# A fused retention, sparse-attention and SwiGLU layer: two low halves of token sums by VectorE instead of by transfer, one gate product on another engine, and denser side work

## The chip, the cores and the metric

The kernel runs on one core of a Trainium2 chip. The metric is the device time of one execution in microseconds (us). The engines are TensorE (PE in the profile; PEld is its weight load), VectorE (DVE), ScalarE (ACT), GpSimd (POOL), and SyncE (SP), which here only issues transfers. Each runs its own instructions in the order in which they were emitted. Transfers run on 16 DMA engines that all queues share.

## What is computed

One layer over 512 tokens of width 1024. The input is projected to the parts of a retention group (rq, rk, rv, rg), of an attention group (aq, ak, av), and of an indexer (iq, ik, iw) that picks the 128 keys of each query. The part that matters here:

```python
proj = x @ w_in
rq, rk, rv, rg, aq, ak, av, iq, ik, iw = jnp.split(proj, IN_SPLITS, axis=-1)
...
ret = retention_chunkwise(rq, rk, rv)             # rope on rq, rk before
ret = ((ret - mu) * lax.rsqrt(var + LN_EPS)).reshape(B, S, RET_WIDTH)
ret = (ret * ret_gn_gain.astype(jnp.float32)).astype(x.dtype)
ret = jax.nn.silu(rg) * ret
...
sel = indexer_topk(iq, ik, iw, topk)
att = sparse_attention(aq, ak, av, sel).reshape(B, S, ATT_WIDTH)
mix = jnp.concatenate([ret, att], axis=-1) @ w_out
x = layer_norm(DEEPNORM_ALPHA * x + mix, ln_mix_gain, ln_mix_bias)
gate, up = jnp.split(x @ w_gate_up, 2, axis=-1)
ffn = (jax.nn.silu(gate) * up) @ w_down
return layer_norm(DEEPNORM_ALPHA * x + ffn, ln_ffn_gain, ln_ffn_bias)
```

## The kernel before

**Number format.** Every large product is made of three matmuls in a rounded 32-bit format: each operand is split into a high half (the rounded value) and a low half (the rest), and `mm3` adds high x high, high x low and low x high (lines 94 to 96). `split` makes the halves. The high half is always a copy on ACT (line 86). The low half is made in one of two ways: an engine that is given subtracts (line 91), or, with `None`, ACT writes the negated source (line 88) and POOL issues a transfer that adds the source to it (line 89, an accumulating transfer of 0.5 MB between two places of SBUF for a half-block).

**Stages.** First the indexer's projection, then sixteen feature projections (`proj_feature`, tiles `pf`), then `token_pair`, which makes rv and rg, then `proj_token` (av, tiles `pt`), then the output projection `mix_part` (tiles `mx`) with attention between its matmuls, layer norm, the FFN in two stages, and the last layer norm.

**`token_pair`.** rv and rg are not projected plainly. Tokens and depth are cut in halves, and seven block products stand for eight: p = 0 to 6 use the token blocks 11, 12, the sums s1, s4, s2, s3, and the block 22, with weight blocks that are sums as well. The products are collected in PSUM tiles X (`ptx`), Z (`ptz`) and Y (`pty`); `after(p, t)` copies or adds a finished one out of PSUM. The fourth product (p = 3) is added in PSUM onto the third (both in Y), behind ACT's copy of the third (line 436).

The token sums are made by `x_sums` on POOL (line 390, four subtractions or additions of 128x1024). `x_split` makes the halves of a sum: s1 and s4 during the feature projections, s2 and s3 during the products p = 2 and p = 3. s2 has its own form with the low half on DVE (lines 405, 406); s1, s4 and s3 go through `split(None, ...)`, that is, by transfer.

**Weights.** `stream` lists the weight blocks; each gives two half-blocks, w0, w1, w2 and so on in order of use: w16 and w17 belong to the first block product, w18 and w19 to the second, and so on up to w28 and w29; w30 to w33 are `proj_token`'s. `weight()` prepares them three ahead. Letters say who makes the low half: V is DVE, G is POOL, Q is the transfer. w16, w17: Q, Q. w18 and w19: V, V. w20 to w25: G and V in turn. w26, w27: G, Q. w28, w29: G, V. Three buffers hold raw blocks, so a load waits until an earlier block has been split. The sums of weight blocks are made by accumulating transfers from memory into a raw block (`from_memory`, line 282), which POOL issues after particular half-blocks have been prepared.

**Side work.** `run(main, *sides)` advances side generators each time the main one yields. `pace(it, r)` gives r units of credit at each yield; a step of a side generator costs what it yields. `side` is the chain of the indexer's rope, its logits, the top-k selections (`topk`, lines 511 and 512: one step is a max of eight and a replacement on DVE; the last block's sixteen steps cost 1.6 units each), the token sums and their splits. `rets` is the list of retention steps; `tail` is its rest and then the first attention block's softmax (`att_score(0)`). During `proj_token` `tail` runs at 1.6 and `side` at 0.8; during the first quarter of the output projection `side` runs at 0.6 and is then drained.

**Retention's gate.** For each of four token blocks b, `gated(b)` applies silu on ACT (line 420) and multiplies by the gain on POOL (line 421); `ret_gate(b)` multiplies the normalised retention by it on POOL (line 638, tile `rzz`); `ret_turn(b)` transposes the result on PE (line 645, tile `rz`) and `put_mix` splits it (lines 559, 560).

**Attention's banks.** The scores of one query block are four PSUM tiles `as` (line 669), read by a DVE reduction each (line 671); the tag has four banks, and the transposes `apt` (line 690) take the next ones in turn.

Of the kernel before, what the change touches and what calls it, by code (L numbers as in the profile page):

```python
# [13 lines left out]
ALU = mybir.AluOpType  # L14
# [39 lines left out]
def hybrid_layer_kernel(ctx: ExitStack, tc: tile.TileContext, xT, x, pos, w0, wf, wt, wo,  # L54
                        wgu, wd, gng, lmg, lmb, lfg, lfb, ident_d, cols_d, masks_d, decay_d, out):
    nc = tc.nc
    V, A, G, T = nc.vector, nc.scalar, nc.gpsimd, nc.tensor
# [9 lines left out]
    def psd(name):  # L67
        return psp.tile([P, 512], F32, tag="d", name=name)
# [7 lines left out]
    def unit(tag, name, dt=F32):  # L76
        return big.tile([P, 4, S], dt, tag=tag, name=name)
# [7 lines left out]
    def split(eng_lo, hi, lo, src):  # L85
        A.copy(hi, src)  # L86
        if eng_lo is None:
            A.activation(lo, src, AF.Copy, scale=-1.0)  # L88
            nc.gpsimd.dma_start(lo.bitcast(F32), src, accum_op=ALU.add)  # L89
        else:  # L90
            eng_lo.tensor_tensor(lo, src, hi.bitcast(F32), op=ALU.subtract)  # L91

    def mm3(acc, lh, ll, rh, rl, first, last, **kw):
        T.matmul(acc, lhsT=lh, rhs=rh, start=first, stop=False, **kw)  # L94
        T.matmul(acc, lhsT=lh, rhs=rl, start=False, stop=False, **kw)  # L95
        T.matmul(acc, lhsT=ll, rhs=rh, start=False, stop=last, **kw)  # L96
# [211 lines left out]
    def weight(ahead=3):  # L308
        k = taken[0]
        taken[0] += 1  # L310
        while len(ready) < min(k + 1 + ahead, 2 * limit[0]):
            prepare()
        return ready[k]
# [6 lines left out]
    gnb = const.tile([P, S], F32, name="gnb")  # L320
# [8 lines left out]
    def settle():  # L329
        while pending:  # L330
            pending.pop(0)()
# [24 lines left out]
    def proj_token():  # L356
        accs = [psd(f"pt{b}") for b in range(NB)]

        def evac(b):
            if b == 0:  # L360
                tok[0] = unit("s4", "av")
            A.copy(tok[0][:, b], accs[b])

        for c in range(4):
            h, l = weight()
            for b in range(NB):
                bs = slice(b * P, b * P + P)
                for k in range(2):
                    kt = 2 * c + k
                    ks = slice(k * S, k * S + S)  # L370
                    mm3(accs[b], xh[kt][:, bs], xl[kt][:, bs], h[:, ks], l[:, ks], kt == 0, kt == KT - 1)
                settle()
                if c == 3:
                    pending.append(lambda b=b: evac(b))
                if b != 1:
                    yield

    xq, xs = {}, {}
# [22 lines left out]
    def x_split(q, tag):  # L401
        xs[q] = big.tile([P, 2, 4, T2], F32R, tag=tag, name=f"x{q}")
        hi, lo = xs[q][:, 0], xs[q][:, 1]
        if q == "s2":
            A.activation(hi, xq["n2"], AF.Copy, scale=-1.0)
            V.scalar_tensor_tensor(lo, in0=xq["n2"], scalar=-1.0, in1=hi.bitcast(F32), op0=ALU.mult, op1=ALU.subtract)
        else:
            split(None, hi, lo, xq[q])

    def x_side(q):  # L410
        if q in ("11", "12", "22"):
# [5 lines left out]
    grg = {}  # L417

    def gated(b):
        A.activation(grg[b], grg[b], AF.Silu)  # L420
        G.tensor_tensor(grg[b], grg[b], gnb, op=ALU.mult)

    def token_pair():
        X = [psd(f"ptx{t}") for t in range(2)]
# [25 lines left out]
        for p, (q, first) in enumerate((("11", True), ("12", True), ("s1", True), ("s4", False), ("s2", False), ("s3", False), ("22", False))):  # L450
            if p == 1:
                d4 = big.tile([P, 4, HEADS * P], F32, tag="s7", name="decay")
                rt["decay"] = d4[:, :2]
                dma(rt["decay"], decay_d)
                grg[2], grg[3] = d4[:, 2], d4[:, 3]
            if p == 2:
                Y += [psd(f"pty{t}") for t in range(2)]
            bank = {1: Z, 2: Y, 3: Y}.get(p, X)
            side_of = x_side(q)
            settle()  # L460
            for u in range(2):
                h, l = weight()
                for t in range(2):
                    for k in range(2):
                        hi, lo = side_of(2 * u + k, t)
                        ks = slice(k * S, k * S + S)
                        mm3(bank[t], hi, lo, h[:, ks], l[:, ks], first and u == 0 and k == 0, u == 1 and k == 1,
                            skip_group_check=True)
                    settle()
                    if u == 1:  # L470
                        pending.append(lambda p=p, t=t: after(p, t))
                    if (p, u, t) == (2, 0, 0):
                        x_split("s2", "s10")
                    elif (p, u, t) == (3, 0, 0):
                        x_split("s3", "s4")
                    yield
# [40 lines left out]
    def chain(*its):  # L517
        for it in its:
            yield from it

    def pace(it, r, credit=0.0):
        while True:
            credit += r
            while credit > 0.0:
                c = next(it, 0.0)
                credit -= 1.0 if c is None else c
                if c == 0.0:
                    break
            yield

    def run(main, *sides):
        for _ in main:
            for s in sides:
                next(s, None)

    def drain(it):
        for _ in it:
            pass
# [109 lines left out]
    def retention():  # L648
        steps = (((ret_keys, 0),), ((ret_score, 0),), ((ret_keys, 1),), ((ret_state, 0),), ((ret_score, 1), (ret_decay, 1)), ((ret_out, 0, 0),),
                 ((ret_out, 0, 1),), ((ret_state, 1),), ((ret_keys, 2),), ((ret_score, 2), (ret_decay, 2)), ((ret_out, 1, 0),),  # L650
                 ((ret_out, 1, 1), (ret_scale, 0)), ((ret_state, 2),), ((ret_score, 3), (ret_scale, 1), (gated, 0)), ((ret_out, 2, 0), (ret_gate, 0)),
                 ((ret_out, 2, 1), (gated, 1)), ((ret_out, 3, 0), (gated, 2), (ret_gate, 1)), ((ret_out, 3, 1), (gated, 3)), ((ret_turn, 0), (ret_scale, 2)),
                 ((ret_gate, 2),), ((ret_turn, 1),), ((ret_scale, 3),), ((ret_gate, 3), (ret_turn, 2)), (), (), ((ret_turn, 3),), ())
        for step in steps:
            for f, *a in step:
                f(*a)
            yield
# [4 lines left out]
    def att_score(b):  # L662
        n = (b + 1) * P
        bias = masks[:, 1] if b == 0 else score[:, b, :n]
        mx = sp.tile([P, 4, 4], F32, tag="mx", name="mx")
        st, ex = [], []
        for h in range(HEADS):
            sc = psu(f"as{b}_{h}")
            T.matmul(sc[:, :n], lhsT=aqT[:, h, b * P:n], rhs=akT[:, h, :n], start=True, stop=True)
            st.append(tmp("ast"))  # L670
            V.tensor_tensor_reduce(out=st[h][:, :n], in0=sc[:, :n], in1=bias, scale=1.0, scalar=-3.0e38,
                                   op0=ALU.add, op1=ALU.max, accum_out=mx[:, 0, h:h + 1])
        V.tensor_scalar(mx[:, 1], mx[:, 0], -ATT_SCALE, None, op0=ALU.mult)
        yield
        for h in range(HEADS):
            A.activation(st[h][:, :n], st[h][:, :n], AF.Exp, scale=ATT_SCALE, bias=mx[:, 1, h:h + 1],
                         accum_out=mx[:, 2, h:h + 1])
        yield
        V.reciprocal(mx[:, 3], mx[:, 2])
        for h in range(HEADS):  # L680
            V.tensor_scalar(st[h][:, :n], st[h][:, :n], mx[:, 3, h:h + 1], None, op0=ALU.mult)
            at[b, h] = st[h]
        yield
# [28 lines left out]
    def x_parts():  # L712
        x_load("s8", "11", "22")
        yield 0.01

    def some(it, n):
        for _ in range(n):
            yield next(it)

    def splits(*a):  # L720
        x_split(*a)
        yield 0.5

    def x_sums_in():
        for _ in x_sums():
            pass
        yield 0.01

    def both(main, it, every):
        for n, c in enumerate(main):  # L730
            yield c
            if n % every == every - 1:
                yield next(it)

    lg1, lg23 = logits(1), chain(logits(2), logits(3))
    side = chain(index_rope(), lg1, both(lg23, tk, 2), x_parts(), some(tk, 3), x_sums_in(), some(tk, 3), splits("s1", "s4"), some(tk, 1), splits("s4", "s6"), tk)
# [5 lines left out]
    def later(it, n):  # L742
        for _ in range(n):
            yield
        yield from it
# [1 line left out]
    run(token_pair(), pace(side, 0.8), later(pace(some(rets, 12), 0.65), 10))  # L747
    mixt[0] = unit("s8", "mrh", F32R), unit("s10", "mrl", F32R)
    tail = chain(rets, att_score(0))
    run(proj_token(), later(pace(tail, 1.6), 1), pace(side, 0.8))  # L750
    drain(tail)


# [885 lines left out]
    for i in range(18):  # L1639
        q, j = WORDER[i]  # L1640
# [97 lines left out]
    b = NB - 1  # L1738
# [82 lines left out]
```

## Time and profile before

| what | value |
|---|---|
| time, median of 3 runs | 618.75 us (618.7 to 619.94) |
| the profiled execution: its own time, its span | 618.67 us, 616.9 us |
| PE busy, PEld busy | 601.8 us (98%), 514.4 us (83%) |
| DVE, ACT, POOL busy | 523.5 us (85%), 372.1 us (60%), 199.5 us (32%) |
| software DMA queue (issued by POOL) | 40.05 MB, 37.3% of the 16 engines' span |
| hardware DMA queue (issued by SP) | 84.10 MB, 38.8% |
| `token_pair` on PE | 124.2 to 177.6 us |
| `proj_token` on PE | 177.6 to 210 us |

A busy share is an average over stages with different limits; what a change in one stage is worth is read from the waits in that stage. In the lists of instructions the first number is the start in us, the second the length in us, and a bracket at the end gives the idle time before the instruction and what ended it. A matmul's end is modelled, so neighbouring matmuls overlap in the list. In the list of waits stand the total, the number and the longest. A view of one tile or line gives the shortest, median and longest duration in ns. A row of a transfer gives who issued it, its size, and the us from issue to landing.

### The profile page before, as it was taken

To read this page: it belongs to the slowest core of one execution; us is meant where nothing else is said; L and a number is where in the kernel's file an instruction comes from. 1 tells how busy PE (TensorE), PEld (TensorE's weight loads), DVE (VectorE), ACT (ScalarE), POOL (GpSimd) and SP (SyncE) were. 2 spreads that over 40 slices of the span, in tenths; PEclk is the share of its full clock that TensorE was granted. 3 is DMA by queue.
4 is the path that set the end of the run, shared out by engine and by line. 5 is a ranking of instruction groups with operands and counts; after the bars stand their busy time and mean duration, and the time that the engine had idled before them with its cause. 6 is when DMAs were issued, how large, how long until landed. Compare 5 with 4: busy or idle time off the path is not lost.

```text
span 616.9 us, 9139 instructions
## 1 busy us (share of the span) xinstructions
PE 601.8 (98%) x3204; PEld 514.4 (83%) x3204; DVE 523.5 (85%) x962; ACT 372.1 (60%) x646; POOL 199.5 (32%) x202
## 2 busy tenths in 40 slices
PE   9999999998999999999999999999999999999995
PEld 6988888876788877889998888888888888688884
DVE  5897798998847897889998999999999898887856
ACT  5645554526484765777657767767776695548300
POOL 1188234956678000232123223132221021214011
PEclk9999999998999999999999999999999999999998
DMA  8799898699894673497399988988876559779602
GB/s 306 280 212 263 207 234 223 151 247 275 199 232 119 265 273 135 109 238 152 120 267 204 242 213 211 230 191 236 199 205 177 139 159 229 187 198 302 202 35 102
DMA packets 45790, 125.98 MB, mean 204 GB/s; under 512 B 4736, under 2 KB 12480, under 8 KB 39984
## 3 DMA queue, kind: packets, MB, share of 16 engines
q1 hardware_dynamic: 25312, 84.10, 38.8%
q0 software_dynamic: 19696, 40.05, 37.3%
q10 hardware_dynamic: 736, 1.25, 0.6%
q8 instruction: 25, 0.41, 0.3%
q14 instruction: 21, 0.17, 0.1%
HBM read 91.30 MB, written 2.10 MB: 151 GB/s over the span
## 4 chain that ended last, share of the span: by engine, by line
PE 81%; DMA 7%; DVE 5%; issue 3%; POOL 2%; ACT 1%; POOLq 0%; SPq 0%; DVEq 0%
PE ga L1050 11%; PE ga L1053 6%; PE gc L1050 5%; PE pf L94 5%; PE pf L95 5%; PE pf L96 5%; PE acc L210 4%; PE gb L1050 3%; PE gc L1053 3%; PE ga L1060 3%; DMA raw<-in_wt_dram 2%; PE mx L96 2%; PE mx L94 2%; PE mx L95 2%; DMA xs<-xqs 2%
## 5 line engine op out<-in xcount | busy, mean ns | idle before, releaser
L86 ACT CAST wh<-raw 128x1024 fp32r<-128x1024 f32 x49 | 51.1, 1049 | 42.0 <-DMA raw<-in_wt_dram 11.8
L94 PE MATMUL pf<-xh,wh 128*128 128x512 f32 x128 | 50.0, 391 | 0.0
L95 PE MATMUL pf<-xl,wh 128*128 128x512 f32 x128 | 49.9, 390 | 0.0
L96 PE MATMUL pf<-xh,wl 128*128 128x512 f32 x128 | 49.8, 389 | 0.0
L549 POOL TENSOR_TENSOR rs<-ve,half 128x1 f32<-128x1 f32 (+1 forms) x11 | 11.8, 1068 | 95.5 <-DVE ve L548 95.4
L91 DVE TENSOR_TENSOR wl<-raw,wh 128x1024 fp32r<-128x1024 f32 x24 | 31.7, 1333 | 8.0 <-ACT wh L86 7.9
L89 POOL DMA_DIRECT2D wl<-raw x20 | 19.2, 961 | 40.2 <-ACT wl L88 40.0
L96 PEld LDWEIGHTS pf<-xh,wl 128*128 128x128 f32 x128 | 24.0, 188 | 5.2
L94 PEld LDWEIGHTS pf<-xh,wh 128*128 128x128 f32 x128 | 24.0, 188 | 4.7
L975 POOL DMA_DIRECT2D firsts<-in_wgu_dram x18 | 21.2, 1191 | 20.7 <-DMA firsts<-in_wgu_dram 20.7
L95 PEld LDWEIGHTS pf<-xl,wh 128*128 128x128 f32 x128 | 24.1, 188 | 4.6
L89 POOL DMA_DIRECT2D slot<-hu x9 | 10.9, 1447 | 50.9 <-ACT slot L88 26.8
L511 DVE MAX8 m<-score 128x8 f32<-128x256 f32 (+2 forms) x48 | 26.6, 555 | 0.6
L512 DVE MATCH_REPLACE8 score<-m,score 128x256 f32<-128x256 f32 (+2 forms) x48 | 26.0, 543 | 0.0
L494 ACT ACTIVATE lg<-lg 128x256 f32<-128x256 f32 (+2 forms) x24 | 10.7, 474 | 21.2 <-PE lg L493 21.1
L88 ACT ACTIVATE wl<-raw 128x1024 fp32r<-128x1024 f32 x20 | 21.2, 1058 | 0.0
L1100 DVE TENSOR_TENSOR gu<-gu,gc 128x512 f32<-128x512 f32 x18 | 12.4, 687 | 8.8 <-ACT gu L1095 8.8
L980 POOL DMA_DIRECT2D graw<-graw x18 | 18.0, 998 | 5.8 <-DVE hu L1104 2.8
L500 DVE SCALAR_TENSOR_TENSOR score<-lg,iw,score 128x256 f32<-128x256 f32 (+2 forms) x21 | 12.9, 615 | 7.5 <-ACT lg L494 6.9
L1095 ACT ACTIVATE gu<-ga 128x512 f32<-128x512 f32 x18 | 10.8, 599 | 14.0 <-PE ga L1053 14.0
L1095 ACT ACTIVATE gt<-ga 128x512 f32<-128x512 f32 (+1 forms) x26 | 13.8, 531 | 5.4 <-PE ga L1060 4.9
L1082 ACT ACTIVATE hu<-hu 128x256 f32<-128x256 f32 x20 | 8.0, 417 | 13.4 <-DVE hu L1072 13.4
(1285 smaller groups left out, 2113.0 us busy)
## 6 DMA issues: line engine op xcount, KB each, us to landing
graw<-in_wgu_dram SPq DMA_DIRECT2D x22, 1024.0 KB, 6.5
wl<-raw POOLq DMA_DIRECT2D x20, 512.0 KB, 7.0
raw<-in_wf_dram SPq DMA_DIRECT2D x8, 1024.0 KB, 8.2
raw<-in_wo_dram SPq DMA_DIRECT2D x8, 1024.0 KB, 5.3
raw<-in_wt_dram SPq DMA_DIRECT2D x7, 1024.0 KB, 6.4
r<-in_wd_dram SPq DMA_DIRECT2D x12, 512.0 KB, 5.6
firsts<-in_wgu_dram SPq DMA_DIRECT2D x18, 256.0 KB, 6.5
firsts<-in_wgu_dram POOLq DMA_DIRECT2D x18, 256.0 KB, 6.2
```

The lines of the kernel that those rows point to most:

```text
L86: A.copy(hi, src)
L89: nc.gpsimd.dma_start(lo.bitcast(F32), src, accum_op=ALU.add)
L91: eng_lo.tensor_tensor(lo, src, hi.bitcast(F32), op=ALU.subtract)
L94: T.matmul(acc, lhsT=lh, rhs=rh, start=first, stop=False, **kw)
L95: T.matmul(acc, lhsT=lh, rhs=rl, start=False, stop=False, **kw)
L96: T.matmul(acc, lhsT=ll, rhs=rh, start=False, stop=last, **kw)
L210: T.matmul(acc0[i][:, o:], lhsT=a[:, i * P:i * P + P], rhs=b[kt][:, o:], start=(kt == 0 and p == 0), stop=(kt == KT - 1 and p == 2))
L511: V.max(m8, a)
L512: V.match_replace(out=a, in_to_replace=m8, in_values=a, imm_value=TAKEN)
L1050: T.matmul(two(gp[n][acc]), lhsT=h[:, ws[k]], rhs=parts[q][:, :, k], start=first and k == 0, stop=False, skip_group_check=True)
L1053: T.matmul(gp[n][acc][:, :Q], lhsT=l[:, ws[k]], rhs=parts[q][:, 0, k], start=False, stop=k == 3, skip_group_check=True)
L1095: A.activation(gp[n][t], gp[n][acc], AF.Copy, scale=-1.0)
```

## The change

Three edits. In `x_split`, s1 and s3 get `split(V, ...)`: DVE subtracts, and ACT's negated copy and the transfer fall away; s4 keeps the transfer. In `gated`, the multiplication of token block 3 goes to DVE. During `proj_token`, `side` runs at 1.0 instead of 0.8.

```diff
@@ x_split
         else:
-            split(None, hi, lo, xq[q])
+            split(V if q in ['s1', 's3'] else None, hi, lo, xq[q])
...
     def gated(b):
         A.activation(grg[b], grg[b], AF.Silu)
-        G.tensor_tensor(grg[b], grg[b], gnb, op=ALU.mult)
+        (V if b in (3,) else G).tensor_tensor(grg[b], grg[b], gnb, op=ALU.mult)
...
     tail = chain(rets, att_score(0))
-    run(proj_token(), later(pace(tail, 1.6), 1), pace(side, 0.8))
+    run(proj_token(), later(pace(tail, 1.6), 1), pace(side, 1.0))
     drain(tail)
```

## The prediction

> **What bounds the kernel now.** I read the busy times by stage first, then what TensorE (PE) waited for, then the single instructions around those waits.
>
> ```profile
> core 0: us, PE busy (x) PEld busy (x) DVE busy (x) ACT busy (x) POOL busy (x), PEclk, DMA share, GB/s
> 124.00:136.10 12.10, 11.26 (x50) 9.02 (x49) 11.61 (x24) 4.14 (x5) 7.74 (x5) 1.00 1.04 221
> 136.10:154.40 18.30, 15.39 (x74) 12.75 (x73) 16.36 (x29) 9.48 (x11) 10.69 (x9) 0.91 1.05 288
> 177.60:210.00 32.40, 31.99 (x177) 27.10 (x176) 20.59 (x60) 19.86 (x39) 18.47 (x19) 1.00 0.60 171
> 210.00:262.00 52.00, 52.00 (x284) 42.82 (x283) 45.30 (x92) 35.06 (x68) 4.45 (x5) 1.00 0.55 192
> ```
>
> PE is the bound: it runs without a gap from 210 to 262 us. Only where the change is made does it lose time, and there (124 to 154 us) the DMA engines are busy all the time and DVE nearly so. The waits of PE in that stretch, longest first:
>
> ```profile
> PE pty L94 <- ACT decay L436: 2.9, 1, 2.9
> PE ptx L95 <- DMA wl<-raw: 0.8, 1, 0.8
> PE ptx L96 <- DMA xs<-xqs: 0.7, 1, 0.7
> PE rz L645 <- POOL rzz L638: 0.4, 1, 0.4
> ```
>
> Three of the four lie in the seven block products, the fourth in the retention tail. So the most that the change can win is in these rows, and PE's own lines around them:
>
> ```profile
> 128.15 0.50 PE L95 MATMUL ptx<-wl,xh 128*128 128x512 f32 x1 [0.84 <-DMA wl<-raw]
> ...
> 146.10 0.80 PE L94 MATMUL pty<-wh,xs 128*128 128x512 f32 x1 [2.91 <-ACT decay L436]
> 146.69 0.63 PE L95 MATMUL pty<-wl,xs 128*128 128x512 f32 x1
> ...
> 149.23 0.39 PE L95 MATMUL pty<-wl,xs 128*128 128x512 f32 x1
> 149.45 0.39 PE L96 MATMUL pty<-wh,xs 128*128 128x512 f32 x1
> ```
>
> Starts of matmuls are 0.22 to 0.23 us apart (149.23, 149.45) while one is shown as 0.39 long, so a gap costs its idle time plus 0.16: here 1.00 and 3.07 us, and the third, 0.69 us by its row further down, 0.85. After the 2.91 us gap the clock drops: from 146.69 to 149.23 six starts take 2.54 us instead of 1.36, and the first one 0.59 instead of 0.23, so the drop costs another 1.54 us. After the 0.84 and 0.69 us gaps it doesn't.
>
> The Trainium skill (TensorE: Matmul & The Clock Gate, What's actually happening) says that the clock falls to half after an idle window of some 3.4 us. Here half clock followed a shorter gap, so the row and the page differ; by the page the 1.54 us would not hang on this gap, which is a rival below.
>
> Why the long gap: PE waits for ScalarE (ACT) to copy the third product (pty) out of PSUM, where the fourth is added, and ACT had been standing before a weight.
>
> ```profile
> 144.50 1.04 ACT L86 CAST wh<-raw 128x1024 fp32r<-128x1024 f32 x1 [2.52 <-DMA raw<-in_wt_dram]
> 145.46 1.08 ACT L436 ACTIVATE decay<-pty 128x512 f32<-128x512 f32 x2
> 134.75 0.88 POOL L282 DMA_DIRECT2D raw<-in_wt_dram x1 [0.30 <-POOL wl L91]
> raw<-in_wt_dram POOLq DMA_DIRECT2D x1, 512.0 KB, 9.7
> wl<-raw POOLq DMA_DIRECT2D x1, 512.0 KB, 8.8
> wl<-raw POOLq DMA_DIRECT2D x1, 512.0 KB, 4.5
> DMA  9999932850599998999999999999999999995089
> q0 software_dynamic: 2304, 8.39, 63.1%
> ```
>
> The weight is half-block w24, whose raw sum is completed by an accumulating transfer issued at 134.75 that took 9.7 us, to 144.4. The transfer of w17's low half (the first wait's cause, issued right behind s1's) took 8.8 us; w16's, which found the engines idle, took 4.5. The last two lines are the DMA view of 100 to 170 us: the digits, one for 1.75 us, stand at 9 from about 121 to 163. The software queue moved 8.39 MB, 16 transfers of 0.52 MB, in 63.1% of 70 us: 2.76 us of all sixteen engines for each.
>
> **The change part by part.** s1 and s3 lose one ACT instruction and one accumulating transfer each, and DVE gets one subtraction each.
>
> ```profile
> 163.08 0.50 PE L96 MATMUL ptx<-wh,xs 128*128 128x512 f32 x1 [0.69 <-DMA xs<-xqs]
> L91 DVE TENSOR_TENSOR wl<-raw,wh x6: 1215/1226/2590, 120.7 to 163.8; 128x1024 fp32r<-128x1024 f32 x6
> ```
>
> Removed: on ACT twice some 1.04 us (an instruction of the size of w24's cast at 144.50), on GpSimd (POOL) twice the issuing of a transfer (0.88 at 134.75), 2 x 2.76 us of DMA. Added: 2 x 1.22 us of DVE by the second row, a subtraction of the same size, or up to 2 x 2.59.
>
> Gain 1: s1's transfer stands in the queue right ahead of w17's low half. Without it that half lands 2.76 us earlier, and 1.00 us of wait was all there was: -1.00. Cover of what is left: w17 has 1.8 us to spare.
>
> Gain 2: everything queued behind s1 moves up as well, as the engines are full, and the w24 sum is among it: up to -3.07 and -1.54. What is left of it follows as cost b.
>
> Gain 3: s3's low half lands at 163.08 and PE waits for it; on DVE it is made right behind w25's low half, some 10 us earlier: -0.85. Late next would be w27's low half, still by transfer behind the same queue; it loses s3's 2.76 us ahead of it, so I cost it at nothing (if it does not move up: up to 1 us).
>
> Cost a: the subtraction of s1 falls where both engines are full.
>
> ```profile
> 112.09 2.41 POOL L390 TENSOR_TENSOR xqs<-xqs 128x1024 f32<-128x1024 f32 x1
> 113.64 0.43 DVE L511 MAX8 m<-score 128x8 f32<-128x256 f32 x1
> 136.22 0.39 PE L94 MATMUL pty<-wh,xs 128*128 128x512 f32 x1
> 129.73 2.35 POOL L226 TENSOR_TENSOR rqT<-rt,rt 128x512 f32<-128x512 f32 x1 [3.58 <-DVE rt L224]
> 132.04 2.40 POOL L91 TENSOR_TENSOR wl<-raw,wh 128x1024 fp32r<-128x1024 f32 x1
> 140.17 2.39 POOL L91 TENSOR_TENSOR wl<-raw,wh 128x1024 fp32r<-128x1024 f32 x1 [3.15 <-ACT wh L86]
> 141.06 2.59 DVE L91 TENSOR_TENSOR wl<-raw,wh 128x1024 fp32r<-128x1024 f32 x1 [1.64 <-ACT wh L86]
> ```
>
> It is emitted ahead of the sixteenth selection step, so it would start at 113.64, inside a POOL sum that ends at 114.50. The last two rows show what then happens: DVE's subtraction that began at 141.06 ended at 143.65, about one length (1.1 us) after POOL's had ended. So I take 0.8 us of waiting and 1.22 of work: DVE is 2.0 us late from there on (bounds: 1.22, and 2.59). DVE has no idle time to absorb it before 139.4 us (the 1.64 us in the last row; 11.61 of 12.10 us busy by the table). POOL waits for DVE's rope at 129.73, and behind that rope on POOL stand the low half of w20 (132.04) and the issue of w24's sum (134.75). Both slide 2.0: w20 is ready at 136.45. PE comes to the third product at 136.22 less gain 1, and reads the low half one matmul later, 135.45: it waits 1.0 us (bounds 0 and 1.6). +1.0.
>
> The Trainium skill (SBUF — State Buffer, Who interferes with whom) calls this port an exclusive lock taken by whoever starts first. If DVE got in between two POOL sums, POOL would pay and DVE be late by 1.22 only: by that reading the time would be some 0.8 us less. The trace shows the lock with DVE as the loser (2.59 instead of 1.22 us); the other order no row here shows.
>
> Cost b: w24's sum is issued at 136.8. It took 9.7 us in a crowded queue and 4.5 is the least a row shows; so it lands between 141.3 and 146.5. I take 141.8, near the lower end: the work ahead of it is shorter by 2.76 us, while it comes 2.0 later, so the queue should be nearly drained when it comes. From landing to PE's matmul there were 1.7 us (144.4 to 146.10), which gives 143.5. PE is there at 146.10 - 3.07 - 1.00 + 1.0 = 143.0: 0.5 us are left, too short to lose the clock. +0.5 (bounds 0 and 5.2).
>
> s3's subtraction, 1.22 to 2.59 us on DVE, is hidden: no row of PE's waits names DVE here, and 1.94 us of DVE are idle from 136.1 to 154.4. If that cover is gone, because PE comes 4 us earlier, the first thing late is retention's scaled keys, by up to 1.2 us; not in the sum, but in the range.
>
> The gate product of token block 3:
>
> ```profile
> 196.30 1.30 POOL L421 TENSOR_TENSOR decay<-decay,gnb 128x512 f32<-128x512 f32 x1
> 197.55 3.53 POOL L638 TENSOR_TENSOR rzz<-rz,decay 128x512 f32<-128x512 f32 x2
> ```
>
> It stands right ahead of the products that PE's fourth wait (0.4 us) hangs on. Without it POOL is 1.3 us earlier there: gain 4, 0.37 + 0.16, about -0.5. On DVE it costs half a 1.22 us subtraction, 0.6, ahead of the low half of the first turned retention block, which PE reads only after 210: nothing.
>
> The pace 1.0 gives 8 selection steps during the token projection instead of 6, and 2 fewer in the output projection. DVE has 32.40 - 20.59 = 11.8 us idle in the first; two steps of 1.5 us are covered (if not, 3 us on retention's chain). In the second DVE is relieved, but PE never waits there: nothing. By the arithmetic of the generators, one step moves, though: from the first softmax's wait to behind it.
>
> ```profile
> 207.95 0.69 DVE L511 MAX8 m<-score 128x8 f32<-128x512 f32 x1
> ...
> 209.76 0.18 DVE L679 RECIPROCAL mx<-mx 128x4 f32<-128x4 f32 x1 [0.33 <-ACT ast L676]
> 210.77 0.42 DVE L671 CUSTOM_DVE_ANT_0 ast<-as,score 128x256 f32<-128x256 f32 x1
> 211.72 0.38 PE L690 MATMUL apt<-ident,ast 128*128 128x128 f32 x2
> ```
>
> The step from 207.95 was done by 209.43, while DVE had to wait for ACT anyway. Now it comes ahead of 210.77 and moves that by 1.48 us; the transpose at 211.72 takes the bank that this reduction (with its 0.42) frees, then at 212.67. Cost c: +0.9 (bounds 0 and 1.5).
>
> Sum: -1.00 - 4.61 - 0.85 - 0.5 + 1.0 + 0.5 + 0.9 = -4.56. The profiled execution took 618.67 (span 616.9), 0.08 under the median of 618.75 shown: 614.1.
>
> **The rivals.** *All waits go, nothing new:* costs a, b and c are 0: 618.67 - 6.96 = 611.7. For it: each cost is a wait that no row shows yet. Against: DVE has no slack ahead of w20.
>
> *The sum of w24 doesn't land earlier, slower:* it keeps its 9.7 us and is issued 2.0 us later, behind DVE and POOL; it lands at 146.5, PE starts at 148.2 instead of 146.10, half clock stays: +2.1 + 0.9 - 0.85 - 0.5 = +1.65, 620.3. It is slower than now once the transfer takes over 8 us. For it: the chain through 129.73 and 134.75 really gets longer. Against: the queue it waited in is what the change empties.
>
> *Half the way, no change:* it takes 7.2 us, lands at 144.0; PE starts at 145.7, the gap is long enough for half clock: -0.4 + 0.9 - 0.85 - 0.5 = -0.85, 617.8.
>
> *The clock drop is not this gap's:* then its 1.54 us stays in the fourth product: 614.1 + 1.54 = 615.6. Against: the drop begins with the first matmul behind the gap; for: the granted clock of that stage, 0.91, doesn't say what it was that lowered it. The rule of the Trainium skill told above speaks for it.
>
> **How the numbers follow.** My forecast 0.58, its own range 612.6 to 616.2 by the bounds of a and c; all waits go 0.13; the clock 0.05; half the way 0.14; slower 0.10. What a measurement here can tell from no change is about 0.2%, 1.2 us, so faster means under 617.5: 0.58 + 0.13 + 0.05 and a part of the half way, 0.78; within 0.13; slower 0.09. The range 611.8 to 617.8 takes in all but the slower rival and the edges of the two outer ones.
>
> **What would show it.** Right: w17's transfer under 7 us and no PE wait in the first product; PE's wait at the start of the fourth under 1 us with matmuls 0.23 apart behind it; no wait for s3; DMA digits below 9 between 121 and 163; small new waits at w20's low half (for POOL) and at the first attention transpose; none at the retention turns. Wrong: DVE or POOL named in waits of over 2 us in the block products, w24's sum still taking over 8 us, or time lost after 262 us, where I expect the same work only earlier.

## The result, and the profile after

The changed kernel takes 615.36 us (median of 5 runs, 613.95 to 616.12), the kernel before 618.7 (5 runs, 617.65 to 619.94): a ratio of 0.9947, interval 0.9927 to 0.9967. The profiled execution took 615.36 us, its span 613.6, so 3.3 less than before; the accounts below are made between the two profiled executions.

The stages first, the same four windows as before (PE, PEld, DVE, ACT and POOL busy us, granted clock, DMA share, GB/s):

```profile
124.00:136.10 12.10, 10.26 (x44) 8.15 (x44) 11.74 (x22) 4.13 (x5) 4.86 (x4) 0.97 1.03 250
136.10:154.40 18.30, 18.02 (x87) 14.86 (x86) 17.89 (x37) 8.63 (x10) 13.09 (x10) 0.92 1.02 251
177.60:210.00 32.40, 31.55 (x175) 26.56 (x175) 23.84 (x70) 19.39 (x40) 15.72 (x15) 1.00 0.62 189
210.00:262.00 52.00, 52.00 (x287) 42.93 (x287) 42.80 (x79) 34.98 (x68) 5.10 (x5) 1.00 0.54 179
```

PE lost 2.9 us of work in the second stage before and loses 0.3 there now, but loses more in the first (10.26 of 12.10 busy, before 11.26), and the low clock has not gone: 0.97 and 0.92, before 1.00 and 0.91. What PE waited for between 95 and 262 us, all of it, and in the last 100 us:

```profile
PE ptz L95 <- DVE wl L91: 1.8, 1, 1.8
PE apt L690 <- DVE mx L671: 0.8, 1, 0.8
PE pty L94 <- ACT decay L436: 0.3, 1, 0.3
...
PE dy L95 <- DVE dlp L91: 0.4, 1, 0.4
```

All four waits shown of before are gone or, at the fourth product, cut from 2.9 to 0.3. Two are new: a low half made by DVE in the second product, and the first attention transpose. PE's own lines at the three places:

```profile
134.45 0.50 PE L95 MATMUL ptz<-wl,xh 128*128 128x512 f32 x1 [1.84 <-DVE wl L91]
...
135.48 0.63 PE L96 MATMUL ptz<-wh,xl 128*128 128x512 f32 x1
...
138.89 0.39 PE L95 MATMUL pty<-wl,xs 128*128 128x512 f32 x1
...
145.90 0.50 PE L94 MATMUL pty<-wh,xs 128*128 128x512 f32 x1 [0.28 <-ACT decay L436]
146.24 0.39 PE L95 MATMUL pty<-wl,xs 128*128 128x512 f32 x1
...
209.45 0.67 PE L690 MATMUL apt<-ident,ast 128*128 128x128 f32 x2 [0.76 <-DVE mx L671]
```

Two things are to be seen. From 135.48 to 138.89 eight starts take 3.41 us instead of 1.81: the half clock that stood behind the fourth product's gap now stands behind the second product's. And the fourth product starts at 145.90, where it started at 146.10: it came 0.2 us earlier, not 3. Its wait is short because PE arrived late.

What made PE late, and when w24 landed (DVE, POOL and ACT in the order of time):

```profile
113.38 1.98 DVE L91 TENSOR_TENSOR xs<-xqs,xs 128x1024 fp32r<-128x1024 f32 x1
114.34 3.27 POOL L390 TENSOR_TENSOR xqs<-xqs,xqs 128x1024 f32<-128x1024 f32 x1
118.16 1.59 POOL L226 TENSOR_TENSOR rqT<-rt,rt 128x512 f32<-128x512 f32 x1
118.24 2.38 DVE L514 TENSOR_SCALAR score<-score 128x256 f32<-128x256 f32 x1
133.17 1.23 DVE L91 TENSOR_TENSOR wl<-raw,wh 128x1024 fp32r<-128x1024 f32 x1
133.22 2.32 POOL L226 TENSOR_TENSOR rqT<-rt,rt 128x512 f32<-128x512 f32 x1 [4.45 <-DVE rt L224]
138.17 0.88 POOL L282 DMA_DIRECT2D raw<-in_wt_dram x1 [0.30 <-POOL wl L91]
144.30 1.05 ACT L86 CAST wh<-raw 128x1024 fp32r<-128x1024 f32 x1 [3.59 <-DMA raw<-in_wt_dram]
145.26 1.08 ACT L436 ACTIVATE decay<-pty 128x512 f32<-128x512 f32 x2
150.74 1.22 DVE L91 TENSOR_TENSOR xs<-xqs,xs 128x1024 fp32r<-128x1024 f32 x1
```

The same two DVE instructions in the kernel before:

```profile
116.63 0.51 DVE L514 TENSOR_SCALAR score<-score 128x256 f32<-128x256 f32 x1
...
129.69 1.23 DVE L91 TENSOR_TENSOR wl<-raw,wh 128x1024 fp32r<-128x1024 f32 x1
```

The subtraction of s1 took 1.98 us. The comparison that closes the first selection (line 514) then came beside POOL's rope and took 2.38 instead of 0.51, so w19's low half, the last row, began 3.48 us later than before. w24's sum was issued at 138.17 instead of 134.75 and landed at 144.30 instead of 144.50 (ACT's cast). Why it landed no earlier, by the two DMA queues from 136 to 138 us (packets, MB, share of the 16 engines), before and after:

```profile
q1 hardware_dynamic: 111, 0.56, 68.7%
q0 software_dynamic: 45, 0.12, 31.1%
```

```profile
q1 hardware_dynamic: 141, 0.75, 106.7%
q0 software_dynamic: 1, 0.00, 0.0%
```

The software queue did empty earlier. By the packets in the traces its backlog ran from 118.36 to 137.97 us before (3.15 MB) and from 118.99 to 135.92 us in the changed kernel (2.62 MB). So it took 2.7 us less, of which 2.05 are left at its end, since the first transfer is issued later (at 117.56 instead of 116.94, behind POOL's sum of 3.27 us). But w24's sum was not in the queue by then: issued at 138.17, it moved its first packet at 139.76, before at 139.41. In between, loads of the hardware queue had the engines.

**The account.** Lost in the block products: before 1.00 + 4.61 + 0.85 = 6.46 us; after 1.84 + 0.16 at w19, 1.60 by the clock, 0.28 + 0.16 at the fourth product, 4.04 in all. That is 2.4 won. By place it is 2.6 (`proj_token` starts at 175.15 us, before 177.78; 0.15 of it lay ahead of the block products): the fourth product's start came 0.2 us forward, the half clock behind it (1.54) and s3's wait (0.85) are gone, and what PE lost ahead of that start cost nothing, since it would have waited there. 0.5 more came at the retention turn, 0.9 was lost at the attention transpose, and some 0.2 I can't place: 2.0 us. The FFN's down projection starts 1.9 us earlier (its first `dx` matmul at 520.27 us, before 522.16). The other 1.4 us arise behind that, where the change touches nothing: the waits of `dy` are 0.4 us there instead of 1.3 (two waits, so 1.06 with the 0.16 for each), and 0.35 I can't name. That wait varies from one profiled execution to the next (0.6 and 0.8 us in two of the kernels below, none in another), so I count it as no effect of the change.

### The profile page after: what moved, and what is told of

Read it like the earlier page. It is cut to its first block, busy times and chain, and to the rows that moved or that the text cites. A ratio compares the mean times of both kernels' runs of the same rounds, so it can differ in the third digit from the quotient of the medians.

```text
span 613.6 us, 9135 instructions
## 1 busy us (share of the span) xinstructions
PE 601.2 (98%) x3204; PEld 514.8 (84%) x3204; DVE 525.8 (86%) x965; ACT 370.5 (60%) x644; POOL 197.2 (32%) x199
## 4 chain that ended last, share of the span: by engine, by line
PE 71%; DVE 13%; DMA 5%; issue 4%; POOL 3%; ACT 2%; POOLq 0%; SPq 0%; DVEq 0%; ACTq 0%
PE ga L1050 11%; PE ga L1053 5%; PE gc L1050 5%; PE acc L210 4%; PE pf L94 4%; PE pf L95 3%; PE pf L96 3%; PE gb L1050 3%; PE gc L1053 3%; PE ga L1060 2%; PE gc L1060 2%; PE dr L96 2%; PE dr L94 2%; PE dr L95 2%; PE gb L1053 1%
## 5 line engine op out<-in xcount | busy, mean ns | idle before, releaser
L549 POOL TENSOR_TENSOR rs<-ve,half 128x1 f32<-128x1 f32 (+1 forms) x11 | 13.1, 1188 | 96.8 <-DVE ve L548 96.5
L91 DVE TENSOR_TENSOR wl<-raw,wh 128x1024 fp32r<-128x1024 f32 x24 | 29.1, 1221 | 7.7 <-ACT wh L86 7.6
L975 POOL DMA_DIRECT2D firsts<-in_wgu_dram x18 | 19.4, 1090 | 20.5 <-DMA firsts<-in_wgu_dram 20.2
```

## Experiments

The theory of the first eight experiments: s1's transfer leaving the queue is the gain in the block products, and DVE's lateness is the cost, which can be won back by moving DVE's work. Three of the eight contradicted it, and the last four went by another: w24's landing, 143 to 145 us, bounds the fourth product, since ACT stands at it before it copies the third; what makes PE earlier turns into waiting there, and what makes it later is free up to that point. Kernels run together are compared through the runs of the kernel before that they share (median 619.0 to 619.3).

**The parts alone.** s1 alone on DVE, pace and gate as before:

```diff
-            split(None, hi, lo, xq[q])
+            split(V if q == 's1' else None, hi, lo, xq[q])
```

> Only s1's low half goes to DVE; s3, the gate product and the pace are as before. Theory (s1's transfer leaving the queue is the whole gain in the block products, DVE's lateness the whole cost): the waits at w17's low half (1.00 us) and at the start of the fourth product (3.07 and 1.54 of half clock) shrink to under 0.6 together, a wait of about 2.0 us at w19's low half appears with some 1.6 us of half clock behind it, and s3's wait (0.85) stays: about 1.6 us faster than before, 617. Rival (the gain comes from s3, the gate and ACT's relief, s1's swap is nothing): 618.7, no change. The wait at w19 must be there in both.

Measured: 618.55 us, ratio 0.9989 (0.9966 to 1.0012): no change, which is the rival's number. Its waits of PE:

```profile
PE ptx L96 <- DMA xs<-xqs: 2.4, 1, 2.4
PE ptz L95 <- DVE wl L91: 1.7, 1, 1.7
PE pty L94 <- ACT decay L436: 0.5, 1, 0.5
PE pty L95 <- POOL wl L91: 0.5, 1, 0.5
```

The lateness of DVE is the one seen above. What was won ahead of s3 is waited away at s3's transfer (2.4 us, before 0.7): the matmul that reads s3's low half started at 162.30 us, before 163.08, though PE had been there 2.5 us earlier, and the half clock came behind this wait, not at w19. So taking out one transfer moved the wait to the next one. s3 alone:

```diff
+            split(V if q == 's3' else None, hi, lo, xq[q])
```

> Only s3's low half goes to DVE. Theory: s3's wait (0.85 us) goes, the two waits ahead of it (w17, fourth product) stay as they were, as s3's transfer is issued after them; no new wait, since DVE has 10 us until the product: 0.9 us faster, 617.8. Rival (s3's transfer was part of what filled the queue, so half of the change's 3.3 us is its doing): 1.5 us or more.

Measured: 616.53 us, 0.9958 (0.9941 to 0.9976): more than the wait of 0.85 us that it takes away.

```profile
PE pty L94 <- ACT decay L436: 3.1, 1, 3.1
PE ptx L95 <- DMA wl<-raw: 1.2, 1, 1.2
```

```profile
146.20 0.50 PE L94 MATMUL pty<-wh,xs 128*128 128x512 f32 x1 [3.11 <-ACT decay L436]
146.54 0.40 PE L95 MATMUL pty<-wl,xs 128*128 128x512 f32 x1
146.78 0.40 PE L96 MATMUL pty<-wh,xs 128*128 128x512 f32 x1
```

Behind a gap of 3.11 us, longer than that of before, the matmuls are 0.23 us apart: in this execution no half clock followed. It is one of three of the twelve runs in which the clock of the whole execution was 0.997, and these three are the fastest (613.79 to 614.61 us; the others, at 0.991 to 0.994, took 615.29 to 618.63). So the clock explains why the profiled execution lies below the median, but not why the median lies 2.5 us below before, 1.6 more than the wait: that stays open, as no profile here shows one of the slower nine. The gate and the pace alone, both splits by transfer:

```diff
-            split(V if q in ['s1', 's3'] else None, hi, lo, xq[q])
+            split(None, hi, lo, xq[q])
```

> The gate product on DVE and the pace of 1.0, both token sums by transfer as before. Theory: the wait at the retention turn (0.4 us) goes, one of about 0.8 us (with 0.16 in starts) appears at the first attention transpose: 0.4 us slower, 619.1, not to be told from before. Rival (denser side work relieves DVE in the output projection and later): faster by 0.5 us or more.

Measured: 619.12 us, 1.0008 (0.9994 to 1.0022). The wait at the retention turn is gone, a wait of 0.8 us at the transpose has come: the two nearly cancel. And the changed kernel with the old pace:

```diff
-    run(proj_token(), later(pace(tail, 1.6), 1), pace(side, 1.0))
+    run(proj_token(), later(pace(tail, 1.6), 1), pace(side, 0.8))
```

> The changed kernel with the pace back at 0.8. Theory: the wait at the first attention transpose (0.76 us) goes and nothing else changes: 0.9 us faster than the changed kernel, 614.4 beside its 615.4. Rival (the denser steps shorten DVE's backlog in the output projection): slower than the changed kernel, 616 or more.

Measured: 613.76 us, 0.9913 (0.9893 to 0.9932), against 0.9947 for the whole change: the transpose's wait is gone, w19's is 2.4 us. The two intervals overlap by a hair, so the size of the difference, some 0.3%, is loose; its sign is what the wait says: the pace is the part of the change that loses time.

**The late comparison of DVE.** The changed kernel with the closing comparison of the first selection put behind the sixth step of the next one:

```diff
+    def close(j):
+        a = score[:, j, :(j + 1) * P]
+        V.tensor_scalar(a, a, TAKEN_EDGE, NEG, op0=ALU.is_gt, op1=ALU.mult)
...
+            if (j, it) == (2, 5):
+                close(1)
...
-        V.tensor_scalar(a, a, TAKEN_EDGE, NEG, op0=ALU.is_gt, op1=ALU.mult)
+        if j > 1:
+            close(j)
```

> The changed kernel with one DVE instruction moved: the closing comparison of the first selection block (2.38 us there, 0.51 before) comes behind the sixth step of the second block, where GpSimd is idle. Theory (DVE loses 2.0 us to s1's subtraction and 1.9 to this comparison, both by waiting for GpSimd): the comparison takes about 0.3 us, w19's low half is ready some 2 us earlier, PE's wait there falls from 1.84 to under 0.4 and the clock stays full; up to 1.0 us of wait appears at w20 (GpSimd): 2 to 3 us faster than the changed kernel, 612.5 to 613.4. Rival (the comparison was long for another reason, such as its data): it stays at 2 us or more wherever it stands, and the time with it.

Measured: 615.02 us, 0.9936 (0.9914 to 0.9957), the same as the whole change.

```profile
128.95 0.28 DVE L508 TENSOR_SCALAR score<-score 128x256 f32<-128x256 f32 x1
...
131.27 1.23 DVE L91 TENSOR_TENSOR wl<-raw,wh 128x1024 fp32r<-128x1024 f32 x1
```

```profile
PE pty L94 <- ACT decay L436: 1.9, 1, 1.9
PE apt L697 <- DVE mx L678: 0.8, 1, 0.8
PE pty L95 <- POOL wl L91: 0.5, 1, 0.5
```

The comparison takes 0.28 us where POOL doesn't hold it up, w19's low half is 1.9 us earlier and PE's wait for it is gone: that it caused the wait is shown. But the 2 to 3 us that the theory expected didn't come. The fourth product's wait is 1.9 us again. It starts at 144.87 us, 1.0 earlier than in the changed kernel, as w24's sum is issued 1.9 us earlier; and the half clock, which there lay ahead of this start, now lies behind it (from 145.41 us). So some 1.0 us of DVE's lateness was not free, the rest was, and in this execution the clock took that 1.0 back.

**The queue.** The changed kernel, with s1's copy and transfer issued as before, into scratch tiles that nobody reads:

```diff
+            if q == "s1":
+                for i in range(2):
+                    t, src = tmp("spare"), xq[q][:, 2 * i:2 * i + 2].rearrange("p k c -> p (k c)")
+                    A.activation(t, src, AF.Copy, scale=-1.0)
+                    nc.gpsimd.dma_start(t, src, accum_op=ALU.add)
```

> The changed kernel, and beside s1's subtraction on DVE the old way is done as well, into scratch that nobody reads: ACT's negated copy and the accumulating transfer, in two halves. Theory (the queue is what the change empties): w17's wait of 1 us comes back, w24's sum lands later again and the fourth product waits 2 us or more with half clock: slower than before, 619 to 621. Rival (it is DVE's and ACT's order that counts, not the queue): as the changed kernel, 615 to 616.

Measured: 620.1 us, 1.0008 (0.9989 to 1.0027): all that the change had won is gone.

```profile
PE pty L94 <- ACT decay L441: 2.4, 1, 2.4
PE ptx L95 <- DMA wl<-raw: 2.3, 1, 2.3
```

```profile
146.98 1.04 ACT L86 CAST wh<-raw 128x1024 fp32r<-128x1024 f32 x1 [3.27 <-DMA raw<-in_wt_dram]
```

The execution shown is the slowest of the twelve (621.97 us). w24's sum is issued as in the changed kernel (138.28 against 138.17) and lands 2.7 us later (146.98 against 144.30), as the software queue's backlog, 3.15 MB again, ends at 139.85 us and not at 135.92. w17's wait is back, and longer than before, since the backlog also starts 1.4 us later than before (119.76 against 118.36): the old transfer together with DVE's lateness is worse than either.

**Issuing w24's sum earlier.** The changed kernel with a pause of 4 units of the side work behind s4's split, so that DVE and POOL have less ahead of it; then the same with the pace at 1.2:

```diff
-    side = chain(..., splits("s4", "s6"), tk)
+    side = chain(..., splits("s4", "s6"), rest(4.0), tk)
```

> The changed kernel with a pause of 4 units of credit in the side work behind s4's split, so three selection steps move from ahead of w19's low half to later. Theory: w19 is ready some 3.7 us earlier, PE's wait there and the half clock go, w20's too; the fourth product waits under 0.6 us; the first attention transpose still waits 0.8: about 3.5 us faster than the changed kernel, 611.9. Rival (DVE is short of time in this stage altogether, so the steps come back as waits for retention's products later): no faster than 614.5.

> As the one with the pause, and the pace during the token projection is 1.2, which puts no selection step behind the first softmax and three into the output projection. Theory: the wait at the first attention transpose goes as well: 611.0. Rival (the ten steps in the token projection hold up retention): a wait at the retention turns or products of 1 us or more, 612 or above.

Measured: 615.81 us, 0.994 (0.9917 to 0.9963), and 615.82, 0.9952 (0.9933 to 0.9972): nothing won, where 611.9 and 611.0 were expected. The rivals' times came, without the waits in retention that they named. w19's wait is gone in both; the fourth product's is 3.4 and 3.1 us. The way of w24's sum through the kernels in which ACT's copy stands behind it, by the packets of the software queue, POOL's issue and ACT's cast; and the start of the half clock, by the trace's record of the granted clock:

| kernel | backlog ends | w24's sum issued | first packet | landed | half clock from |
|---|---|---|---|---|---|
| before | 137.97 | 134.75 | 139.41 | 144.50 | 145.76 |
| s3 alone | 138.76 | 134.62 | 139.36 | 144.60 | none |
| gate and pace alone | 137.72 | 134.14 | 138.87 | 144.07 | 145.16 |
| s1 alone | 136.13 | 137.81 | 139.40 | 143.40 | 162.36 |
| changed | 135.92 | 138.17 | 139.76 | 144.30 | 135.46 |
| changed, old pace | 137.70 | 138.57 | 140.16 | 144.77 | 134.50 |
| changed, comparison late | 136.34 | 136.29 | 138.72 | 143.27 | 145.41 |
| changed, pause | 136.85 | 135.37 | 139.40 | 143.80 | 146.12 |
| changed, pause, pace 1.2 | 136.43 | 134.78 | 138.80 | 143.43 | 145.71 |
| changed, transfer put back | 139.85 | 138.28 | 142.29 | 146.98 | 129.44 and 149.92 |
| last kernel below, s4 on DVE too | 130.64 | 136.70 | 138.28 | 142.12 | none |

In every row the fourth product starts 1.6 us behind the landing. What holds the sum back differs. With s1's transfer in the queue (the first three rows, and where it is put back) the backlog ends at 137.7 us or later, and hardware-queue loads, 99 to 101% of the engines, come between it and the sum. Without it, in four kernels (s1 alone, changed, old pace, the last) the sum comes into an empty software queue and its first packet follows 1.6 us behind the issue: there the issue decides, so POOL does, and DVE ahead of it. Where it is issued earlier (comparison late, the two pauses), the first packet takes 2.4 to 4.0 us, and from the end of the backlog until then the hardware queue has the engines to 101%. That its loads hold the sum up is my reading; no run moves them. They also moved 2.54 MB ahead of w24's first packet in the changed kernel, before 1.90. So without s1's transfer the two limits lie close together: an issue 2.8 and 3.4 us earlier than the changed kernel's lands 0.5 and 0.9 us earlier, and in both kernels with the pause the half clock came right behind the fourth product's start (145.39 and 145.03 us).

**ACT's order.** In the kernel before, w24 and w25 prepared one call later, so that ACT copies the third product before it stands at w24's cast; nothing else changed:

```diff
-                h, l = weight()
+                h, l = weight(2 if (p, u) == (2, 1) else 3)
```

> The kernel before, with one edit: w24 and w25 are prepared one call later, so ACT copies the third product out of PSUM before it stands at w24's sum. Theory (the fourth product's wait is ACT standing at w24, whose sum lands at 143 to 145 us in every kernel so far): that wait goes, but s3's low half still lands at about 163 by transfer, so PE's wait there grows by what it won, from 0.7 to 4 us or more: 618 to 619, no change. Rival (s3's transfer is paced by PE and comes earlier with it): 615 or below.

Measured: 621.41 us, 1.0043 (1.0024 to 1.0063): slower, and 2.4 us above the expectation's upper end.

```profile
PE ptx L96 <- DMA xs<-xqs: 3.2, 1, 3.2
PE ptx L95 <- POOL wl L91: 1.4, 1, 1.4
PE ptx L94 <- ACT grg L441: 1.0, 1, 1.0
```

The fourth product no longer waits, and PE waits longer later, for s3's transfer above all (before 0.7), with half clock there for 6.83 us from 161.42. The same edit on the kernel with pause and pace 1.2, and on before with s3 and the gate on DVE, s1 by transfer, pace 0.8:

> The kernel with the pause and the pace of 1.2, and w24 and w25 prepared one call later. Theory: its only large wait, 3.1 us at the fourth product, and the half clock behind it go, and the next limit, w24's own use some 7 us later, is not reached: 3.5 to 4.7 us faster than without that edit, 611 to 612.3. Rival (everything behind w24's sum in the queue is as late, so PE waits for w24 or w26 instead): 614 or more, with a wait of over 2 us in the fifth or sixth product.

> The kernel before with s3's low half and the gate product on DVE and w24, w25 prepared one call later; s1 stays with the transfer, pace 0.8. Theory: waits of 1.0 us at w17 stay, the fourth product's and s3's and the retention turn's go, no lateness of DVE; w24's low half, made on GpSimd behind a load that landed at 146, is next with 0 to 2 us: 612.5 to 614.5. Rival (s1's transfer must leave the queue for any of this to count): 616 or more.

Measured: 614.16 us, 0.9924 (0.9903 to 0.9946), and 613.96, 0.9923 (0.9903 to 0.9943). The second stayed within what the theory gave: with s1's transfer still in the queue, s3's split, the gate and the order of ACT's work took less time than the whole change did. The first is 2 us above its theory, at its rival's time. The first one's stages and waits:

```profile
124.00:136.10 12.10, 12.10 (x55) 10.04 (x54) 11.66 (x25) 4.13 (x5) 7.82 (x6) 1.00 1.03 237
136.10:154.40 18.30, 18.30 (x100) 15.60 (x99) 17.92 (x35) 8.94 (x11) 11.05 (x9) 1.00 1.05 274
```

```profile
PE ptx L94 <- ACT grg L441: 1.8, 1, 1.8
PE pt L95 <- DMA wl<-raw: 1.0, 1, 1.0
PE apt L690 <- DVE mx L671: 0.3, 1, 0.3
```

PE runs through both stages without a gap, 30.4 of 30.4 us, and then waits 1.8 us at 158.22 us in the sixth product, for the next copy that ACT makes behind a weight (its cast began at 156.63 us, when the weight's load had landed). The limit has moved to a later weight.

**More work out of the queue.** The kernel with the pause (now 6 units) and pace 1.2, with s4 on DVE as well:

```diff
-            split(V if q in ['s1', 's3'] else None, hi, lo, xq[q])
+            split(V, hi, lo, xq[q])
```

> The kernel with the pause and the pace of 1.2, with s4's low half on DVE as well and the pause at 6 units. Theory (the DMA engines do a fixed amount of work ahead of w24's sum without a gap, so its landing moves by what is taken out): the sum lands 2 to 2.8 us earlier, at about 141, and the fourth product's wait falls from 3.1 to about 1 us; 2 to 4 us faster than with s4 by transfer, 612 to 614. Rival (the landing is set by when the engines start, or by GpSimd's issue): it stays at 143 us or later and so does the time.

Measured: 612.87 us, 0.991 (0.9888 to 0.9932), the lowest time of all kernels here.

```profile
142.12 1.05 ACT L86 CAST wh<-raw 128x1024 fp32r<-128x1024 f32 x1 [4.04 <-DMA raw<-in_wt_dram]
```

Without s4's transfer, and with the longer pause, w24 lands 1.3 us earlier than with it (143.43), where 2 to 2.8 were expected: the backlog ends 5.8 us earlier, but the sum is issued at 136.70 us, and that is the limit now. The fourth product waits 0.4 us instead of 3.1. No wait of PE's in the block products is over 0.5 us. What this kernel and the other ACT order would give together was not tried.

## Why the prediction was right, and where it wasn't

The median came out at 615.36 for a forecast of 614.1, inside the forecast's own range; the profiled execution won 3.3 us of 4.56, and 1.4 of these 3.3 come from a place that the sum didn't name, which is luck. So the sum proper was 4.56 predicted, 2.0 found, and 1.5 of the 2.0 hang on where the half clock falls, which differs between executions. By its terms:

- **Gain 1** (1.00): right about the wait, which is gone and comes back with the transfer; but it lies ahead of a start that hardly moved, so it won nothing of its own.
- **Gain 2** (4.61): the step that failed, together with cost b. It let w24's sum move up with the queue and land at 141.8. The software queue did move up, by 2.05 us, and was empty when the sum came, as the prediction said. But the sum was issued at 138.17 for 136.8 and took 6.0 us for 5.0, so w24 landed 0.2 us earlier than before and the fourth product started 0.2 us earlier, for 3.07 predicted. An earlier issue alone would have won about 1 us more (144.87 and 145.03 with the late comparison and the pause at pace 1.2), since the first packet then waits while loads of the hardware queue, which the sum left out, have the engines. The fourth product's wait shrank because PE came 2.4 us later than before (145.62 for 143.19). The 1.54 of the half clock did come, though not because the queue let go: the episode fell into the second product, ahead of a start that hardly moved, and cost nothing there. So 1.7 of 4.61.
- **Gain 3** (0.85): the wait is gone, but the term was too small: with s1 already on DVE, leaving s3 to its transfer costs 2.4 us of waiting, as s1 alone shows, and s3 alone won 2.5 us. Without s3's, s1's split wins nothing.
- **Gain 4** (0.5): right; the wait is gone with gate and pace alone, too.
- **Cost a** (1.0): the subtraction's 2.0 us was right to the second digit (1.98), by the lock as described. Missing was the next victim: the comparison behind it slid beside POOL's rope and lost another 1.87 us, so DVE was 3.5 late and PE waited 2.0 (1.84 and 0.16) for a low half of DVE's own, w19, not 1.0 for POOL's w20. The order of which the prediction said that no row shows it is shown now: POOL's sum at 114.34 began while DVE held on, and took 3.27 us instead of 2.41. Here the Trainium skill agrees (SBUF — State Buffer, Who interferes with whom): a `tensor_scalar` can take the shared port too, and whoever starts second stands still for the whole instruction. What PE waited at w19 lay ahead of the fourth product's start and was free; what the lateness cost is the late issue of w24's sum, 3.4 us behind that of before where 2.0 were forecast, worth some 1.0 us by the late comparison's kernel.
- **Cost b** (0.5): 0.44 measured, but by two errors that cancel: landing at 144.30 for 141.8, and PE later than forecast.
- **Cost c** (0.9): 0.92 measured (0.76 and 0.16), and gone with the old pace.
- **Hidden at nothing**: s3's subtraction (1.22 us at 150.74) and the extra selection steps are, with no wait behind them.

Of the rivals, "half the way" had the mechanism nearest to what happened (w24 landing at 144.0), and its start of 145.7 is the one found (145.90). Its 617.8 was too high by the half clock, which it left behind that start, and by the 1.4 us in the down projection. The rival by which the clock drop is not this gap's fell: in the kernel before the half clock begins at 145.76 us, inside the gap, which ends at 146.10.

## What to carry to other kernels

In a stretch where the transfer engines are full, taking one transfer out brings forward what is already queued behind it. The transfer that matters gains by that only if it is issued in time, and if the other queue's loads don't take the engines first: look at both queues and at the issue. A wait that shrinks because the waiter came late has won nothing by itself: compare the start of the instruction behind it, not the wait. And where DVE and POOL share work, an instruction that is 2 us late can meet another's lock and be 3.5 late, so follow the slid chain one instruction further than the one that was added.

## What the runs showed of the hardware

**Half clock comes in windows of fixed place, and about half a window of idle PE is enough.** In the record of the granted clock all stretches that end within the fourteen executions are whole multiples of 3.413 us: 139.946 us of full clock before (41), 129.706 changed (38), 604.159 with s3 alone (177), 3.413 of half clock each time, or 6.827. So the windows run on whatever PE does, and their place against the kernel's start differs between executions. A window's clock follows PE's idle time in the window before it:

| kernel | idle time in one window | next window |
|---|---|---|
| before | 2.57 of the gap of 2.91 | half |
| changed | 1.84, all of its gap | half |
| changed, comparison late | 1.93, all of its gap | half |
| before, copy first | 1.72, two gaps | half |
| s1 alone | 1.74, all of its gap at w19 | full |
| s3 alone | 1.46 and 1.65, the gap of 3.11 cut in two | full |

The other half clocks in the block products and at s3's wait followed 1.98 us of idle time or more, and every other window up to 600 us had under 1.4 and full clock behind it. The border lies at 1.7 to 1.8 us, about half a window; the two rows next to it are in the wrong order by 0.02, within what modelled matmul ends allow. Where an episode stood behind a gap that PE could not avoid, it cost 1.5 to 1.6 us. The Trainium skill (TensorE: Matmul & The Clock Gate, What's actually happening) gives a free-running window of 3413 ns, and the length and the free running agree. That an idle window of some 3.4 us is needed doesn't agree with these rows.

**A comparison of 128x256 on DVE took 0.28 and 0.51 us, and 2.38 where it began beside a `tensor_tensor` of POOL's**; POOL paid likewise beside DVE's subtraction, 3.27 us for 2.41.

**An accumulating transfer of 0.5 MB moved its first packet 1.6 us after its issue where its queue was empty** (four kernels), and 2.4 to 4.0 us after it where the hardware queue had the engines to 101%. How the engines choose between the two queues no run here tells.
